# Filling the rotated key columns by a copy at the head of a step, and scaling all 96 key columns on VectorE

## The chip, the cores and the metric

The kernel runs on one core of a Trainium2 chip. Time is the device time of one execution in microseconds (us). Before the change three runs gave 1371.18, 1371.32 and 1372.91 us, a median of 1371.32. Engines are named as in the profile: PE is TensorE's matmul, PEld its weight load, DVE is VectorE, ACT is ScalarE, POOL is GpSimd, and SP is SyncE, which issues the DMAs here.

## The reference

One layer of a mixer: three attention branches and a gate over 2048 tokens of width 1024. The change touches the keys of the latent attention (MLA) alone: 8 heads, each key with 64 columns of its own and 32 rotary columns that all heads share.

```
q  = (rms_norm(cq, q_norm_g) @ w_uq)    # 8 heads x 96
kv = (rms_norm(ckv, kv_norm_g) @ w_ukv) # 8 heads x (64 key + 64 value)
k  = concat([k_nope, k_rope])           # k_rope: 32 columns, one copy for all heads
q, k = rms_norm(q, qn_g), rms_norm(k, kn_g)         # over the 96 columns
q, k = (rope on the last 32 columns of each)
o  = softmax(q k^T / sqrt(96), causal) v
```

The norm divides a whole key by one number, so the rotation of the 32 shared columns can be done once, ahead of the division. What is left for each head and token is to multiply 96 columns by the inverse root: 64 columns that the head owns, and 32 that are the same for all heads up to this factor.

## The kernel before, in words

The work is cut into blocks of 512 tokens (four tiles of 128) and into steps. A step is one block for one group of heads: first the memory branch (m), then the differential branch (d), then the latent branch (a). The sixteen latent steps are named a00 to a33: the first digit is the group of two heads, the second the block of queries.

`prep_a` prepares such a step. Four tiles of matmuls (L838, L842) make q, k and v in PSUM; ACT brings q and the 64 key columns to SBUF (L844, L845), ACT and DVE bring v there. ACT squares, DVE sums the squares (L854, L857) and multiplies the 64 key columns by a gain (L858). POOL then rotates 32 columns of q in place (`rope_in_place`, L354 to L358), adds the sum of squares of the rotary part (L862), adds epsilon (L97) and raises to the power -0.5 (L101); the result is `r_a`, the inverse roots of q and k. POOL also makes the tables for the rotation of the following step (L332 to L335, tile `rt_a`).

With `r_a` the keys are scaled in two pieces: POOL multiplies the shared rotated columns `krot` by the root and writes columns 64 to 95 of the tile `kn_a` (L867), DVE multiplies columns 0 to 63 in place (L871). DVE scales q too (L873). ACT then rounds k and q to f16 (L878, L885), DVE takes the remainder (L879, L886), and SP sends both through a transposing DMA to `kT_a` and `qB_a`, head by head. PE needs these for a first pass that estimates the row maxima (`est_block`, L398) and then for the scores (L917 to L919), whose exponentials ACT makes (L506) and whose low halves DVE makes (L507).

The tiles `kn_a` and `sqq_a` (squares, and space for the rotation) share two buffers, tag `t4`.

Every generator yields costs, and a planner at the end of the function picks the piece that is due next. That sets priorities; a scheduler then decides the order on each engine. Each engine takes its instructions in that order, so one that waits holds up all behind it. Fill work (gates, the output projection of the finished branches, L958 to L961) is spread between the steps in the same manner.

Of the kernel before, what the change touches and what calls it, by code (L numbers as in the profile page):

```python
# [16 lines left out]
ALU = mybir.AluOpType  # L17
# [15 lines left out]
def _bc(ap, axis, n):  # L33
    ap = ap.unsqueeze(axis)
    shape = list(ap.shape)
    shape[axis] = n
    return ap.broadcast_to(shape)
# [3 lines left out]
def hybrid_block(ctx: ExitStack, tc: tile.TileContext, x, mem, positions, norm_g, w_in, mla_q_norm_g,  # L41
# [3 lines left out]
    V, A, G, T, SP = nc.vector, nc.scalar, nc.gpsimd, nc.tensor, nc.sync  # L45
# [15 lines left out]
    def bigt(shape, name):  # L61
        return big.tile(shape, F16, tag="big", name=name)
# [28 lines left out]
    def rstd_of(ss, shape, name, tag="rstd", eps=EPS):  # L91
        r = sm.tile([P, 32 if tag == "rstd" else 8], F32, tag=tag, name=name)
        n = int(np.prod(shape))
        rv = r[:, 0:n]
        if len(shape) == 2:
            rv = rv.rearrange("p (a b) -> p a b", b=shape[1])
        G.tensor_scalar(rv, ss, eps, None, ALU.add)  # L97
        m = mhalf
        if len(shape) == 2:
            m = m.unsqueeze(2)  # L100
        G.tensor_tensor(rv, rv, m.broadcast_to([P] + list(shape)), ALU.pow)  # L101
        return rv
# [96 lines left out]
    def new_qkv(name):  # L199
        return wk.tile([P, 4, 256], F32, tag="qkv", name=name, bufs=2)  # L200

    def tmp4(name):
        return wk.tile([P, 1024], F32, tag="t4", name=name, bufs=2)
# [122 lines left out]
    def rope_tabs(b, g, name):  # L326

        tb = wk.tile([P, 2, 4, 32], F32, tag="rtab", name=f"rt_{name}", bufs=1)
        c = cos_t[:, 4 * b:4 * b + 4, :]
        s = sin_t[:, 4 * b:4 * b + 4, :]  # L330
        g1, g2 = _bc(g[:, 0:16], 1, 4), _bc(g[:, 16:32], 1, 4)
        G.tensor_tensor(tb[:, 0, :, 0:16], c, g1, ALU.mult)  # L332
        G.tensor_tensor(tb[:, 0, :, 16:32], c, g2, ALU.mult)
        G.tensor_tensor(tb[:, 1, :, 0:16], s, g2, ALU.mult)
        G.tensor_tensor(tb[:, 1, :, 16:32], s, g1, ALU.mult)  # L335
        return tb
# [12 lines left out]
    def rope_in_place(q, tb, nh, eng, tmp):  # L349

        tmp = tmp.rearrange("p (t h d) -> p t h d", t=4, d=32)
        C = _bc(tb[:, 0], 2, nh)
        Sn = _bc(tb[:, 1], 2, nh)
        eng.tensor_tensor(tmp[..., 0:16], q[..., 16:32], Sn[..., 0:16], ALU.mult)  # L354
        eng.tensor_tensor(tmp[..., 16:32], q[..., 0:16], Sn[..., 16:32], ALU.mult)
        eng.tensor_tensor(q, q, C, ALU.mult)
        eng.tensor_tensor(q[..., 0:16], q[..., 0:16], tmp[..., 0:16], ALU.subtract)
        eng.tensor_tensor(q[..., 16:32], q[..., 16:32], tmp[..., 16:32], ALU.add)  # L358
# [8 lines left out]
    def put_v(vt, ps):  # L367

        A.activation(vt[:, :, 0:64], ps, AF.Copy, scale=1.0 / WS)
        V.scalar_tensor_tensor(vt[:, :, 65:129], ps, 1.0 / WS, vt[:, :, 0:64], ALU.mult, ALU.subtract)  # L370
# [339 lines left out]
    krot, ss_kr = [], []  # L710
# [108 lines left out]
    def new_v(b, nm):  # L819
        if b in AB:  # L820
            return bigt([P, 4, 2, 130], f"V_{nm}")
        return kvp.tile([P, 4, 2, 130], F16, tag="V", name=f"V_{nm}", bufs=5)

    def prep_a(st):
        g, b, nm = st.g, st.b, st.name
        tb = rope_tabs(b, g_q[:, 64:96], nm)
        q = new_qkv(f"qkv_{nm}")[:, :, 0:192].rearrange("p t (h d) -> p t h d", d=96)
        knt = tmp4(f"kn_{nm}")
        kn = knt[:, 0:768].rearrange("p (t h d) -> p t h d", t=4, d=96)
        vt = new_v(b, nm)  # L830
        G.memset(vt[:, :, :, 64:65], WS)
        for t in range(4):
            ps = ps_p.tile([P, 512], F32, tag="pp", name="pp")
            q0, k0 = 192 * g, 256 * g
            first = True
            for c in range(2):
                for hx, hw in ((0, 0), (0, 1), (1, 0)):
                    T.matmul(ps[:, 0:192], lhsT=lat_q[b][:, t, hx, c, :], rhs=wuq[c][:, hw, q0:q0 + 192], start=first,  # L838
                             stop=False, skip_group_check=True)
                    first = False  # L840
            for i, (hx, hw) in enumerate(((0, 0), (0, 1), (1, 0))):
                T.matmul(ps[:, 192:448], lhsT=lat_kv[b // 2][:, b % 2, t, hx, :], rhs=wukv[0][:, hw, k0:k0 + 256],  # L842
                         start=False, stop=(i == 2), skip_group_check=True)
            A.activation(q[:, t], ps[:, 0:192].rearrange("p (h d) -> p h d", d=96), AF.Copy, scale=1.0 / WS)  # L844
            A.activation(kn[:, t, :, 0:64], ps[:, 192:320].rearrange("p (h d) -> p h d", d=64), AF.Copy, scale=1.0 / WS)  # L845
            put_v(vt[:, t], ps[:, 320:448].rearrange("p (h d) -> p h d", d=64))
            yield 1.6
        sqt = tmp4(f"sqq_{nm}")
        sq = sqt[:, 0:768].rearrange("p (t h d) -> p t h d", t=4, d=96)
        ss = sm.tile([P, 2, 8], F32, tag="ssa", name=f"ss_{nm}")  # L850
        for i, m in enumerate((sqt, knt)):
            sk = m[:, 768:1024].rearrange("p (t h d) -> p t h d", t=2, d=64)
            A.activation(sk, kn[:, 2 * i:2 * i + 2, :, 0:64], AF.Square, scale=1.0 / math.sqrt(96))
            V.reduce_sum(ss[:, 1, 4 * i:4 * i + 4], sk.rearrange("p t h d -> p (t h) d"), axis=AX.X)  # L854
        A.activation(sq, q, AF.Square, scale=1.0 / math.sqrt(96))
        yield 1.0
        V.reduce_sum(ss[:, 0, :], sq.rearrange("p t h d -> p (t h) d"), axis=AX.X)  # L857
        V.tensor_tensor(kn[..., 0:64], kn[..., 0:64], _bc(_bc(g_n, 1, 2), 1, 4), ALU.mult)  # L858
        yield 1.0
        rope_in_place(q[..., 64:96], tb, 2, G, sqt[:, 768:1024])  # L860
        s4 = ss[:, 1, :].rearrange("p (t h) -> p t h", h=2)
        G.tensor_tensor(s4, s4, _bc(ss_kr[b], 2, 2), ALU.add)  # L862
        r = rstd_of(ss.rearrange("p a b -> p (a b)"), [16], f"r_{nm}")
        rq = r[:, 0:8].rearrange("p (t h) -> p t h", h=2)
        rk = r[:, 8:16].rearrange("p (t h) -> p t h", h=2)
        yield 1.0
        G.tensor_tensor(kn[..., 64:96], _bc(krot[b], 2, 2), _bc(rk, 3, 32), ALU.mult)  # L867
        yield 1.0
        yield 1.0
        yield 1.0  # L870
        V.tensor_tensor(kn[..., 0:64], kn[..., 0:64], _bc(rk, 3, 64), ALU.mult)  # L871
        yield 1.0
        V.tensor_tensor(q, q, _bc(rq, 3, 96), ALU.mult)  # L873
        kT = bigt([P, 2, 4, 2, P], f"kT_{nm}") if b in AB else kvp.tile([P, 2, 4, 2, P], F16, tag="kT", name=f"kT_{nm}")
        st.qs, st.qB = [], []
        for h in range(2):
            ks = stack([P, 4, 2, P], f"ks{h}_{nm}")
            A.activation(ks[:, :, 0, 0:96], kn[:, :, h], AF.Copy)  # L878
            lo = V.tensor_tensor(ks[:, :, 1, 0:96], kn[:, :, h], ks[:, :, 0, 0:96], ALU.subtract)  # L879
            with tc.issue_after(lo.ins):  # L880
                V.memset(ks[:, :, :, 96:128], MS)
            SP.dma_start_transpose(kT[:, h].rearrange("p t l k -> p (t l) k"), ks.rearrange("p t l d -> p (t l d)"))
            yield 1.0
            qs = stack([P, 2, 4, P], f"qs{h}_{nm}")
            A.activation(qs[:, 0, :, 0:96], q[:, :, h], AF.Copy)  # L885
            lo = V.tensor_tensor(qs[:, 1, :, 0:96], q[:, :, h], qs[:, 0, :, 0:96], ALU.subtract)  # L886
            with tc.issue_after(lo.ins):
                V.memset(qs[:, :, :, 96:128], 0.0)
            st.qs.append(qs)
            st.qB.append(new_qb([P, 2, 4, P], f"qB{h}_{nm}"))  # L890
            SP.dma_start_transpose(st.qB[h].rearrange("p l t k -> p (l t) k"), qs.rearrange("p l t d -> p (l t d)"))
            yield 1.0
        st.kTs = st.prev.kTs + [kT] if b else [kT]
        st.Vs = st.prev.Vs + [vt] if b else [vt]
        yield 1.0
        yield 1.0
        for h in range(2):
            yield from est_block(st, h, 1, lambda m: st.qs[h][:, 0, :, 96], lambda m, t: st.qB[h][0:96, 0, t, :],
                                 lambda m, c, n: st.kTs[c][0:96, h, 0:n, 0, :])
            SP.dma_start_transpose(st.qB[h][:, 0], st.qs[h][:, 0].rearrange("p t d -> p (t d)"))  # L900
            ready.add((nm, h))
            yield 1.0
# [361 lines left out]
```

## Time and profile before

| what | value |
|---|---|
| median of three runs | 1371.32 us |
| time of the profiled execution | 1372.15 us |
| its span, first to last instruction | 1370.3 us |
| PE busy | 1293.0 us, 94% |
| DVE busy | 1123.1 us, 82% |
| ACT busy | 903.9 us, 66% |
| POOL busy | 333.9 us, 24% |
| mean granted clock of TensorE | 0.989 |

The profiled execution lies 0.83 us above the median, and 1.85 us of it lie outside the span. A busy share is a mean over stages: the latent steps with their preparation lie between about 640 and 1220 us, and the tail after that has no POOL work at all.

### The profile page before, as it was taken

How to read it: one execution, taken by the hardware profiler on the slowest of the kernel's cores; microseconds unless marked ns; L12 is line 12 of the kernel's file. 1: busy time of each engine (PE TensorE's matmuls, PEld its weight loads, DVE VectorE, ACT ScalarE, POOL GpSimd, SP SyncE). 2: the span in 40 equal slices, each digit the busy share in tenths (PEclk: the TensorE clock that was granted, in tenths of full speed). 3: DMA queues.
4: the chain of work that ended last, by engine and by line, in shares of the span. 5: the costliest groups of instructions: out<-in, count | busy, mean ns of one | idle time of the engine just before them, and what ended most of it. 6: DMA issues, size and time to landing. Idle time of an engine off the chain costs nothing.

```text
span 1370.3 us, 35041 instructions
## 1 busy us (share of the span) xinstructions
PE 1293.0 (94%) x13616; PEld 829.5 (61%) x13616; DVE 1123.1 (82%) x2713; ACT 903.9 (66%) x2163; POOL 333.9 (24%) x477
## 2 busy tenths in 40 slices
PE   5988999999999999999998999999999998999998
PEld 2434556667667767667775656666655665655554
DVE  4657888879889867889899889999998998886745
ACT  6656544677878646786896667677766877665521
POOL 2322232403042133113202143223243323200000
PEclk9999999999999999999999999999999999999999
DMA  7998844223113322447446166347525643275452
GB/s 231 199 208 184 184 111 101 59 60 88 41 25 71 79 34 60 78 110 193 124 98 144 40 167 150 84 107 167 109 71 118 145 99 55 40 155 158 141 184 70
DMA packets 294262, 155.52 MB, mean 113 GB/s; under 512 B 239952, under 2 KB 272848, under 8 KB 294096
## 3 DMA queue, kind: packets, MB, share of 16 engines
q1 hardware_dynamic: 294064, 153.29, 47.7%
q8 instruction: 106, 1.74, 0.5%
q14 instruction: 60, 0.49, 0.1%
q0 software_dynamic: 32, 0.00, 0.0%
HBM read 61.75 MB, written 34.34 MB: 70 GB/s over the span
## 4 chain that ended last, share of the span: by engine, by line
PE 56%; DVE 13%; POOL 9%; ACT 8%; DMA 8%; issue 4%; SPq 1%; ACTq 0%; DVEq 0%; POOLq 0%
PE pp L189 6%; PE pp L187 6%; PE pp L188 6%; PE pe L398 5%; DVE plo L507 4%; PE pv L518 3%; PE pv L516 3%; PE pv L536 3%; PE st L572 3%; PE pp L958 3%; PE pp L959 3%; PE pp L960 3%; PE st L917 3%; PE st L918 2%; PE st L919 2%
## 5 line engine op out<-in xcount | busy, mean ns | idle before, releaser
L506 ACT ACTIVATE p<-st 128x512 f32<-128x512 f32 (+3 forms) x672 | 356.2, 551 | 167.2 <-PE st L919 65.8
L507 DVE TENSOR_TENSOR plo<-p 128x512 f16<-128x512 f32 (+3 forms) x672 | 404.6, 615 | 63.1 <-ACT p L506 59.2
L407 ACT ACTIVATE ec<-pe 128x512 bf16<-128x512 f32 (+3 forms) x384 | 197.2, 536 | 39.2 <-PE pe L400 17.1
L516 PEld LDWEIGHTS <-p 128*128 128x128 bf16 x2304 | 186.0, 99 | 51.5 <-DVE y_a L924 4.7
L518 PEld LDWEIGHTS <-p 128*128 128x128 bf16 x2304 | 173.1, 98 | 39.4 <-issue 4.1
L408 DVE TENSOR_TENSOR er<-er,ec 128x512 bf16<-128x512 bf16 (+3 forms) x384 | 141.5, 378 | 29.9 <-ACT ec L407 15.2
L404 ACT ACTIVATE er<-pe 128x512 bf16<-128x512 f32 x192 | 110.0, 606 | 47.2 <-DVE mx_a L413 18.1
L536 PEld LDWEIGHTS <-plo 128*128 128x128 f16 x2304 | 123.1, 97 | 23.7 <-DVE plo L507 5.8
L917 PE MATMUL st<-qB_a,kT_a 97*128 97x512 f16 (+1 forms) x320 | 112.8, 353 | 13.6 <-ACT p L506 8.7
L516 PE MATMUL pv<-V_d,p 128*128 128x65 f16 x1088 | 116.8, 194 | 3.3 <-DVE y_d L579 2.9
L189 PEld LDWEIGHTS <-ht_x 128*128 128x128 f16 x896 | 87.7, 98 | 52.9 <-ACT ht_x L137 3.9
L188 PEld LDWEIGHTS <-ht_x 128*128 128x128 f16 x896 | 87.8, 98 | 47.8 <-issue 4.0
L518 PE MATMUL pv<-V_d,p 128*128 128x64 f16 x1088 | 116.5, 196 | 0.0
L572 PE MATMUL st<-qB_d,kT_d 97*128 97x512 f16 (+1 forms) x320 | 111.4, 353 | 5.2 <-ACT zc L704 2.1
L187 PEld LDWEIGHTS <-ht_x 128*128 128x128 f16 x896 | 87.7, 98 | 47.1 <-issue 2.8
L516 PE MATMUL pv<-V_a,p 128*128 128x65 f16 x1088 | 112.6, 193 | 2.0 <-DVE y_a L924 1.9
L918 PE MATMUL st<-qB_a,kT_a 96*128 96x512 f16 (+1 forms) x320 | 112.6, 352 | 0.0
L398 PE MATMUL pe<-kT_d,qB_d 96*128 96x512 f16 (+2 forms) x320 | 106.2, 348 | 6.8 <-ACT ec L407 3.6
L518 PE MATMUL pv<-V_a,p 128*128 128x64 f16 x1088 | 112.2, 195 | 0.0
L919 PE MATMUL st<-qB_a,kT_a 96*128 96x512 f16 (+1 forms) x320 | 111.9, 350 | 0.0
L398 PE MATMUL pe<-kT_a,qB_a 96*128 96x512 f16 (+2 forms) x320 | 100.0, 349 | 7.7 <-DMA qB_a<-qs_a 4.6
L189 PE MATMUL pp<-w_d,ht_x 128*128 128x512 f16 x256 | 97.0, 379 | 0.0
(293 smaller groups left out, 3337.7 us busy)
## 6 DMA issues: line engine op xcount, KB each, us to landing
xt_x<-in_x_dram SPq DMA_DIRECT2D x16, 512.0 KB, 4.7
xr<-in_x_dram SPq DMA_DIRECT2D x16, 512.0 KB, 3.6
part<-xr SPq DMA_DIRECT2D x16, 512.0 KB, 2.9
ysc<-yt SPq DMA_DIRECT2D x31, 256.0 KB, 2.3
yl<-ysc SPq DMA_DIRECT2D x15, 512.0 KB, 4.6
zsc<-zc SPq DMA_DIRECT2D x48, 128.0 KB, 2.1
xa<-part SPq DMA_DIRECT2D x12, 512.0 KB, 3.6
out_dram<-xa SPq DMA_DIRECT2D x12, 512.0 KB, 2.9
```

Of the source, the lines that this page charges most:

```text
L187: T.matmul(ps[:, :n], lhsT=ht[:, 0, k], rhs=wt[:, 0, :n], start=(k == 0), stop=False)
L188: T.matmul(ps[:, :n], lhsT=ht[:, 0, k], rhs=wt[:, 1, :n], start=False, stop=False)
L189: T.matmul(ps[:, :n], lhsT=ht[:, 1, k], rhs=wt[:, 0, :n], start=False, stop=(k == NK - 1))
L398: T.matmul(ps[:, 0:n], lhsT=lhs(m, t), rhs=rhs(m, c, n // P), start=True, stop=c < b)
L407: A.activation(ec[:, 0:n], ps[:, 0:n], AF.Copy)
L506: A.activation(p32[:, :n], ps[:, :n], AF.Exp, scale=self.scale)
L507: V.tensor_tensor(plo[:, :n], p32[:, :n], phi[:, :n], ALU.subtract)
L516: T.matmul(pvv[:, t, 0:65], lhsT=phi[:, c], rhs=vt[:, 0:65], start=(j == 0 and t == 0), stop=False, skip_group_check=True)
L518: T.matmul(pvv[:, t, 0:64], lhsT=phi[:, c], rhs=vt[:, 65:129], start=False, stop=False, skip_group_check=True)
L536: last["pv"] = T.matmul(pvv[:, t, 0:65], lhsT=plo[:, c], rhs=vt[:, 0:65], start=False, stop=(j == self.njt - 1), skip_group_check=True)
L572: T.matmul(ps[:, :n], lhsT=st.kTs[j // 4][0:97, h, j % 4, m % 2, :], rhs=st.qB[h][0:97, t0:4, m % 2, :], start=True, stop=not diag)
L917: T.matmul(ps[:, :n], lhsT=kt[0:97, h, j % 4, 0, :], rhs=q[0:97, 0, t0:4, :], start=True, stop=False)
```

## The change

POOL no longer multiplies. At the head of a step, behind the memset of the column of ones of v, it copies the 32 rotated columns into columns 64 to 95 of `kn_a` for both heads of the group. Once the roots are there, DVE multiplies all 96 columns in one instruction.

```
         vt = new_v(b, nm)
         G.memset(vt[:, :, :, 64:65], WS)
+        G.tensor_copy(kn[..., 64:96], _bc(krot[b], 2, 2))
         for t in range(4):
...
         yield 1.0
-        G.tensor_tensor(kn[..., 64:96], _bc(krot[b], 2, 2), _bc(rk, 3, 32), ALU.mult)
-        yield 1.0
-        yield 1.0
-        yield 1.0
-        V.tensor_tensor(kn[..., 0:64], kn[..., 0:64], _bc(rk, 3, 64), ALU.mult)
+        yield 1.0
+        yield 1.0
+        yield 1.0
+        V.tensor_tensor(kn, kn, _bc(rk, 3, 96), ALU.mult)
```

The copy is L832 of the changed kernel. Lines from 833 to 866 of the changed kernel are those of before plus one (L862 is L863 there), and from L871 on the numbers are the same again.

The first place is POOL in step a02, from the end of the rotation of q to the roots. `kn_a03` is the key tile of the next step, `rt_a03` its rotation tables, `V_a` tiles of later values. Before:

```order
L358 TENSOR_TENSOR qkv_a02_13501<-qkv_a02_13501,sqq_a02_13667 128x4x2x16
L332 TENSOR_TENSOR rt_a03_14184<-cos_t_113,g_q_119 128x4x16
L333 TENSOR_TENSOR rt_a03_14184<-cos_t_113,g_q_119 128x4x16
L334 TENSOR_TENSOR rt_a03_14184<-sin_t_114,g_q_119 128x4x16
L335 TENSOR_TENSOR rt_a03_14184<-sin_t_114,g_q_119 128x4x16
L862 TENSOR_TENSOR ss_a02_13668<-ss_a02_13668,sskr2_7324 128x8
L831 MEMSET V_a12_16203 128x8
L97 TENSOR_SCALAR r_a02_13735<-ss_a02_13668 128x16
L101 TENSOR_TENSOR r_a02_13735<-r_a02_13735,mhalf_97 128x16
L831 MEMSET V_a20_17646 128x8
L867 TENSOR_TENSOR kn_a02_13502<-krot2_7357,r_a02_13735 128x8x32
```

The same stretch of POOL in the changed kernel:

```order
L358 TENSOR_TENSOR qkv_a02_13501<-qkv_a02_13501,sqq_a02_13668 128x4x2x16
L332 TENSOR_TENSOR rt_a03_14184<-cos_t_113,g_q_119 128x4x16
L333 TENSOR_TENSOR rt_a03_14184<-cos_t_113,g_q_119 128x4x16
L334 TENSOR_TENSOR rt_a03_14184<-sin_t_114,g_q_119 128x4x16
L335 TENSOR_TENSOR rt_a03_14184<-sin_t_114,g_q_119 128x4x16
L863 TENSOR_TENSOR ss_a02_13669<-ss_a02_13669,sskr2_7324 128x8
L832 COPY kn_a03_14190<-krot3_7698 128x8x32
L97 TENSOR_SCALAR r_a02_13736<-ss_a02_13669 128x16
L831 MEMSET V_a12_16203 128x8
L101 TENSOR_TENSOR r_a02_13736<-r_a02_13736,mhalf_97 128x16
L831 MEMSET V_a20_17646 128x8
```

The multiplication behind the roots is gone, and the copy for step a03 stands ahead of the roots of step a02. It stands so (the copy for the next step ahead of L101 of this one) in eleven of the sixteen steps: a00 to a21, and a32. In a22, a23, a30, a31 and a33 no copy stands in that stretch.

The second place is DVE around the scaling in the same step; `plo` are low halves of exponentials, `xr` rows of the output projection, `rl` and `y_d` belong to the end of a differential step. Before:

```order
L507 TENSOR_TENSOR plo_13705<-p32_13704 128x512
L526 RECIPROCAL rl_13752<-pv_13099 128x4
L871 TENSOR_TENSOR kn_a02_13502<-kn_a02_13502,r_a02_13735 128x8x64
L873 TENSOR_TENSOR qkv_a02_13501<-qkv_a02_13501,r_a02_13735 128x4x192
L507 TENSOR_TENSOR plo_13744<-p32_13743 128x384
L581 TENSOR_SCALAR rl_13752<-rl_13752,neglam_132 128x4
L879 TENSOR_TENSOR ks0_a02_13805<-kn_a02_13502,ks0_a02_13805 128x4x96
```

DVE in the changed kernel:

```order
L507 TENSOR_TENSOR plo_13679<-p32_13678 128x128
L961 SCALAR_TENSOR_TENSOR xr3_13693<-pp_13770,xr3_13693 128x512
L871 TENSOR_TENSOR kn_a02_13502<-kn_a02_13502,r_a02_13736 128x768
L873 TENSOR_TENSOR qkv_a02_13501<-qkv_a02_13501,r_a02_13736 128x4x192
L507 TENSOR_TENSOR plo_13706<-p32_13705 128x512
L526 RECIPROCAL rl_13753<-pv_13100 128x4
L879 TENSOR_TENSOR ks0_a02_13805<-kn_a02_13502,ks0_a02_13805 128x4x96
```

L871 is one instruction over 768 elements instead of 512, and the low half and the reciprocal that stood ahead of it now stand behind L873. Small moves of this kind run through the order of PE, ACT and DVE over all latent steps, and the fill work moves with them.

## Rows read from the trace of the kernel before

**Rows 1.** The page, busy time by engine (us, share of the span, instructions).

```profile
PE 1293.0 (94%) x13616; PEld 829.5 (61%) x13616; DVE 1123.1 (82%) x2713; ACT 903.9 (66%) x2163; POOL 333.9 (24%) x477
```

**Rows 2.** Windows: stretch, length, busy (instructions) by engine, granted clock, DMA share, GB/s.

```profile
core 0: us, PE busy (x) PEld busy (x) DVE busy (x) ACT busy (x) POOL busy (x), PEclk, DMA share, GB/s
640.00:1220.00 580.00, 546.14 (x6394) 364.58 (x6393) 524.51 (x1291) 425.09 (x1040) 162.59 (x223) 0.98 0.48 111
1220.00:1370.00 150.00, 144.64 (x1270) 78.29 (x1266) 89.64 (x183) 54.52 (x107) 0.00 (x0) 1.00 0.47 143
745.00:775.00 30.00, 24.91 (x384) 17.68 (x382) 26.36 (x72) 23.73 (x58) 0.13 (x1) 0.89 0.27 47
1035.00:1050.00 15.00, 12.46 (x106) 6.83 (x105) 11.17 (x27) 6.59 (x17) 6.84 (x10) 0.77 0.66 94
```

**Rows 3.** Waits of PE, 640 to 1370 us: total us, times, longest us.

```profile
PE st L917 <- ACT p L506: 8.7, 13, 2.5
PE pe L398 <- DMA qB_a<-qs_a: 4.6, 3, 2.0
PE st L917 <- DMA qB_a<-qs_a: 4.3, 4, 1.5
```

**Rows 4.** Chain that ended last, 786 to 800 us (step a02): start us, us, what.

```profile
787.09 2.94 POOL r_a L101
790.04 0.02 issue
790.06 0.04 DVE kn_a L871
...
790.67 1.22 DVE qkv_a L873
...
795.84 3.50 DMA qB_a<-qs_a
...
799.39 0.66 PE pe L398 x3
```

**Rows 5.** Timeline of POOL, 783.5 to 791.5 us: start us, us, instruction [idle].

```profile
784.18 0.91 POOL L358 TENSOR_TENSOR qkv_a<-qkv_a,sqq_a 128x128 f32<-128x128 f32 x1
...
786.40 0.19 POOL L862 TENSOR_TENSOR ss_a<-ss_a,sskr 128x8 f32<-128x8 f32 x1
...
786.75 0.26 POOL L97 TENSOR_SCALAR r_a<-ss_a 128x16 f32<-128x16 f32 x1
787.09 2.94 POOL L101 TENSOR_TENSOR r_a<-r_a,mhalf 128x16 f32<-128x16 f32 x1
...
790.11 1.12 POOL L867 TENSOR_TENSOR kn_a<-krot,r_a 128x256 f32<-128x256 f32 x1
```

**Rows 6.** Timeline of DVE in the same step.

```profile
790.06 0.69 DVE L871 TENSOR_TENSOR kn_a<-kn_a,r_a 128x512 f32<-128x512 f32 x1 [0.39 <-POOL r_a L101]
790.67 1.37 DVE L873 TENSOR_TENSOR qkv_a<-qkv_a,r_a 128x768 f32<-128x768 f32 x1
```

**Rows 7.** Timeline of DVE in step a23, with POOL idle.

```profile
1054.50 0.95 DVE L873 TENSOR_TENSOR qkv_a<-qkv_a,r_a 128x768 f32<-128x768 f32 x1
```

**Rows 8.** Lines: group, count, busy us, mean ns, idle before and its releaser.

```profile
L873 DVE TENSOR_TENSOR qkv_a<-qkv_a,r_a 128x768 f32<-128x768 f32 x16 | 19.2, 1201 | 0.0
...
L867 POOL TENSOR_TENSOR kn_a<-krot,r_a 128x256 f32<-128x256 f32 x16 | 17.5, 1096 | 0.9
...
L871 DVE TENSOR_TENSOR kn_a<-kn_a,r_a 128x512 f32<-128x512 f32 x16 | 11.7, 730 | 7.1 <-POOL r_a L101 7.0
...
L462 POOL MEMSET s_d<- 128x256 f16 x32 | 9.5, 310 | 60.9 <-DVE zc L705 16.1 <-DMA qB_m<-qa_m 16.0 <-issue 10.6
```

**Rows 9.** Source L867: shortest, median and longest of its instructions, in ns.

```profile
L867 POOL TENSOR_TENSOR kn_a<-krot,r_a x16: 728/1122/1328, 682.0 to 1183.9; 128x256 f32<-128x256 f32 x16
```

**Rows 10.** Source L332, the first of the table products: shortest, median, longest, ns.

```profile
L332 POOL TENSOR_TENSOR rt_a<-cos_t,g_q x16: 318/700/777, 628.3 to 1138.2; 128x64 f32<-128x64 f32 x16
```

**Rows 11.** Waits of ACT, 640 to 1370 us: total us, times, longest us.

```profile
ACT ks_a L878 <- POOL kn_a L867: 13.2, 10, 3.0
```

## The prediction

> **What bounds the kernel now.** I read the busy times first: PE is busy for 1293.0 of 1370.3 us, DVE for 1123.1, POOL for 333.9 [rows 1]. So time is lost where PE waits or where its clock is low, and the question is whether the edited chain does either. The windows come second [rows 2]. From 640 to 1220 us, where all sixteen latent steps are prepared, PE is busy for 546.1 of 580 us and DVE for 524.5; in the tail POOL does nothing, so the edit can't act there except by what it leaves behind. [...] At full speed the windows would have taken 30 x 0.11 = 3.3 us and 15 x 0.23 = 3.5 us less.
>
> Third, the waits of PE [rows 3]: 4.6 us in three waits of the estimate (L398) for the transposed queries, 4.3 us in four waits of the scores for the same DMA, and 8.7 us in thirteen waits for exponentials, the longest 2.5 us. These 17.6 us are all that a shorter or longer preparation can act on directly. The chain of waits shows one such place whole, step a02 [rows 4]: roots on POOL, L871 and L873 on DVE, then ACT and DVE work, the DMA of `qB_a` and the estimate on PE at 799.39. There, what comes before L101 counts in full. The timeline of POOL [rows 5] shows that POOL works without a pause from the rotation (L358) to the roots: what is put in between makes the roots late by its own length.
>
> **What the change removes.** L867 ran right behind the roots, beside L871 and L873. The timelines show that this cost DVE time: L871 takes 0.69 us, POOL's L867 starts 0.05 us after it and takes 1.12 us, and L873, which starts while L867 runs, takes 1.37 us [rows 5, 6]; with POOL idle the same L873 takes 0.95 us [rows 7]. Alone L867 takes 0.73 us, its median is 1.12 [rows 9]. So the first to start goes at its own pace and the other waits for it. [...]
>
> The sum on DVE: L873 has a mean of 1.201 us over sixteen [rows 8], so the collisions cost it 16 x (1.201 - 0.945) = 4.1 us, which go. L871 grows from 512 to 768 elements. That is the shape of L873, so 0.945 us instead of a mean of 0.730 [rows 7, 8]: 16 x 0.215 = 3.4 us, which come. DVE gains 0.7 us, which is nothing among 1123.
>
> On the path behind the roots, in a02: before, keys were ready when L867 ended, 791.23, that is 1.17 us after L871 started, and queries when L873 ended, 1.98 us after it. Afterwards keys need 0.95 us and queries 0.95 + 0.95 - 0.08 (the overlap of the two rows) = 1.82 us. So both come 0.2 us sooner after the roots.
>
> **What the change adds.** A copy of 128x256 per step. It is not shown in this trace. It must take at least as long as a memset of as many elements, which reads nothing, 0.31 us [rows 8], and at most as long as L867, which reads twice, 0.73 us alone and 1.12 us in its median with DVE beside it [rows 9]. I take the middle of the two undisturbed values, 0.52, and add something for collisions: of the small table products that stand in the same stretch of POOL the shortest takes 0.32 and the median 0.70 us [rows 10]; half of this difference gives 0.7 us in all. [...]
>
> The place decides more than the length. The buffers make it: the next step's `kn_a` takes the buffer in which q was just rotated, so its copy can't start before L358 of this step. In the new order of POOL it therefore stands, in eleven of sixteen steps, between the tables and L101, ahead of the roots of the step before. Queued behind it are L97 and L101, and for them wait L871 on DVE (7.0 us of waiting already [rows 8]) and all that stands behind L871. So in eleven steps keys and queries come 0.7 - 0.2 = 0.5 us later than before; in the other five 0.2 us sooner. The bounds per step are 0.31 - 0.2 = +0.1 and 1.12 - 0.2 = +0.9 us.
>
> What of it reaches the end? If all of it did: 11 x 0.5 - 5 x 0.2 = +4.5 us. If PE always had other work: nothing. PE waited for the transposed queries before an estimate three times [rows 3], and I count those three: +1.5 us, with bounds of 3 x 0.1 = +0.3 and 11 x 0.9 - 1.0 = +8.9 us. In the other steps the cover is fill work of the output projection and the preceding scores on PE; where that cover is used up the step counts too. The ACT wait for L867, 13.2 us in ten waits [rows 11], isn't a gain of its own: it now ends with L871, by the same roots, and is in the sum by the 0.2 us.
>
> Against the profiled execution, 1372.15 us, this is 1373.6; that execution lies 0.83 us above the median of the three runs, and a median goes into the forecast: 1371.32 + 1.5 = 1372.8 us.
>
> **Rivals.** First, faster. The key side no longer needs POOL, the collision at L873 is gone, and ACT, whose exponentials stand behind L878, is held up less. For a gain beyond the 0.2 us per step one of the low-clock places must go: at 1035 to 1050 us PE waits up to 2.5 us for exponentials and 3.5 us are lost to the clock [rows 2, 3]. Step a22 is prepared there, one of the five with no copy ahead of its roots. Price: 1371.3 - 2.5 - 3.5 = 1365.3 us, or with 0.5 to 1.5 us of late roots elsewhere about 1366.5. For it: the windows show the spot; against it: 0.2 us is small against 2.5, so only the moved order could do it.
>
> Second, slower. Late roots add a long PE wait and a low-clock stretch. Its place is a02: PE waits at the end of the chain in rows 4, and the wait grows by the copy. From the point where a wait is followed by a low clock, as beside 752 us (PE waits 2.0 us [rows 3], clock 0.89 [rows 2]), it costs 3.3 to 3.5 us more. Time: 1372.8 + 3.4, and one more step on the path with 0.5 to 1 us, about 1377. For it: eleven delayed steps and DVE, which stands in order behind the roots, at 90% in this stage; against it: only three of sixteen estimates waited at all.
>
> Third, nothing: the copy is short, both 0.2 us savings meet it, and PE covers the rest: 1371.3 us. It shares its outcome with my forecast.
>
> The order of the fill work moves on PE, DVE and ACT over all steps. That is not a term that I can sum; it acts by waits and low-clock spots of the size above, in either direction, and is why the range is wider than the sum.
>
> **How the numbers follow.** A change is told from none at about 0.2%, 2.7 us: faster is below 1368.6, slower above 1374.1. My forecast together with the third rival gets 0.38 (within 0.2%). Slower, by late roots or by order, gets 0.34. Faster gets 0.28. The likeliest case's own range is 1370 to 1375. The range 1367.0 to 1379.0 reaches to 1366.5 of the first rival almost and past 1377 of the second, and takes in most of the +0.3 to +8.9 us of the sum; about 0.1 is left out on each side.
>
> **What would show it.** Right: L873 at 0.95 us in every step; L871 at about 0.95; the copy at 0.5 to 0.9 us between the tables and L97; ACT's L878 released by L871 on DVE; DVE's wait at L871 for the roots up from 7.0 us to 10 or more; the PE wait for `qB_a` longer by about 0.5 us at a02. Wrong: a copy of 1.1 us or more, or L871 slowed beyond 1 us by another POOL read, would mean a collision that I priced too low; DVE waits at L871 no longer than before would mean that the order made room for the copy, and the first or third rival holds. If the count of low-clock stretches between 640 and 1220 us changes, the size comes from order and not from the terms above.

## The result, and the profile after

The changed kernel takes 1386.66 us in the median of four runs (1383.81 to 1388.34), the kernel before 1372.12 us beside it: a ratio of 1.0097 with an interval of [1.0068, 1.0126]. It is slower, by about 14 us, and outside the range of the forecast. The profiled execution took 1386.20 us with a span of 1384.5, so it stands for the median.

Busy times hardly move. The page of the changed kernel, answering to [rows 1]:

```profile
PE 1298.9 (94%) x13616; PEld 832.6 (60%) x13616; DVE 1121.5 (81%) x2713; ACT 903.2 (65%) x2163; POOL 325.7 (24%) x477
```

DVE has 1.6 us less to do, POOL 8.2 us less, and PE 5.9 us more of busy time for the same matmuls, at a mean granted clock of 0.984 (0.989 before). The windows of the changed kernel, with the columns of [rows 2]:

```profile
640.00:1220.00 580.00, 539.25 (x6265) 360.50 (x6262) 510.85 (x1261) 412.71 (x1017) 157.41 (x222) 0.97 0.47 108
1220.00:1370.00 150.00, 148.34 (x1394) 82.87 (x1391) 95.11 (x207) 67.30 (x133) 0.00 (x0) 1.00 0.47 140
745.00:775.00 30.00, 24.72 (x374) 17.27 (x371) 26.46 (x71) 23.54 (x57) 0.00 (x0) 0.89 0.31 50
1035.00:1050.00 15.00, 15.00 (x177) 9.65 (x175) 14.96 (x36) 10.16 (x24) 6.84 (x10) 1.00 0.64 130
1100.00:1200.00 100.00, 89.08 (x1021) 56.55 (x1021) 85.34 (x216) 70.58 (x164) 26.23 (x34) 0.91 0.36 72
```

In the latent stage, 640 to 1220 us, PE does 6.9 us less in the same 580 us than before, DVE 13.7 us less, and the clock is 0.97 for 0.98. Of the two spots that the forecast had marked, 745 to 775 us is as before (a granted clock of 0.89). In 1035 to 1050 us PE now runs without a pause at a clock of 1.00 (0.77 before), but the kernel is some 9 us late by then (counted in matmuls), and a spot like it comes later: from 1055 to 1075 us the clock is 0.83 (1.00 before). In the 100 us from 1100 it is 0.91, so 9 us of full-speed work are lost in that stretch alone; before it was 0.97 there, 3 us.

Waits of PE in the changed kernel, 640 to 1370 us, as in [rows 3]:

```profile
PE st L917 <- ACT p L506: 11.3, 13, 2.4
PE pe L398 <- ACT ec L407: 7.2, 12, 1.3
PE st L917 <- DMA qB_a<-qs_a: 6.5, 4, 2.4
PE pe L398 <- DMA qB_a<-qs_a: 3.7, 3, 2.5
```

The estimate's wait for the transposed queries, on which the forecast rested, went from 4.6 to 3.7 us. At a02, where the forecast had looked for 0.5 us more, it fell from 1.29 to 0.55 us (PE's timeline, before and after):

```profile
799.39 0.66 PE L398 MATMUL pe<-kT_a,qB_a 96*128 96x512 f16 x3 [1.29 <-DMA qB_a<-qs_a]
```

```profile
804.28 0.66 PE L398 MATMUL pe<-kT_a,qB_a 96*128 96x512 f16 x3 [0.55 <-DMA qB_a<-qs_a]
```

The waits for exponentials (8.7 to 11.3), of the scores for queries (4.3 to 6.5) and of the estimate for its own copies on ACT (1.3 us in four before, now 7.2 in twelve) grew.

What the edit does to its own instructions came out close to what was worked out. Its three lines as groups (as in [rows 8]), and the copy's shortest, median and longest in ns (as in [rows 9]):

```profile
L871 DVE TENSOR_TENSOR kn_a<-kn_a,r_a 128x768 f32<-128x768 f32 x16 | 15.8, 985 | 14.9 <-POOL r_a L101 14.9
L873 DVE TENSOR_TENSOR qkv_a<-qkv_a,r_a 128x768 f32<-128x768 f32 x16 | 15.7, 981 | 0.0
...
L832 POOL COPY kn_a<-krot 128x256 f32<-128x256 f32 x16 | 10.9, 683 | 0.0
```

```profile
L832 POOL COPY kn_a<-krot x16: 388/540/1159, 634.8 to 1155.0; 128x256 f32<-128x256 f32 x16
```

L873 fell from 1.201 to 0.981 us, L871 grew to 0.985, the copy's median is 0.54 us, its mean 0.68. The wait of DVE for the roots doubled, from 7.0 to 14.9 us. POOL in step a02, answering to [rows 5]:

```profile
788.29 0.90 POOL L358 TENSOR_TENSOR qkv_a<-qkv_a,sqq_a 128x128 f32<-128x128 f32 x1
...
790.73 0.40 POOL L832 COPY kn_a<-krot 128x256 f32<-128x256 f32 x1
791.21 0.32 POOL L97 TENSOR_SCALAR r_a<-ss_a 128x16 f32<-128x16 f32 x1
...
791.65 2.93 POOL L101 TENSOR_TENSOR r_a<-r_a,mhalf 128x16 f32<-128x16 f32 x1
```

The copy stands between the rotation (L358) and the roots (L101), as the order had it. And ACT's L878 now waits for L871, about as long as it waited for L867 [rows 11]:

```profile
ACT ks_a L878 <- DVE kn_a L871: 12.3, 10, 3.3
```

So the edited instructions did what was expected, and the sum was still wrong. Two explanations were tested: "late roots" (the copies make the roots late, and the end sees it) and "order" (the edit makes the scheduler put other work in another place, and that costs).

### The profile page after: what moved, and what is told of

The parts are those of the page before. It is cut to its first block, busy times and chain, and to the rows that moved or that the text cites. A ratio compares the mean times of both kernels' runs of the same rounds, so it can differ in the third digit from the quotient of the medians.

```text
span 1384.5 us, 35034 instructions
## 1 busy us (share of the span) xinstructions
PE 1298.9 (94%) x13616; PEld 832.6 (60%) x13616; DVE 1121.5 (81%) x2713; ACT 903.2 (65%) x2163; POOL 325.7 (24%) x477
## 4 chain that ended last, share of the span: by engine, by line
PE 52%; DVE 14%; DMA 10%; POOL 9%; ACT 8%; issue 5%; SPq 1%; ACTq 0%; DVEq 0%; POOLq 0%
PE pp L187 6%; PE pp L189 6%; PE pp L188 6%; PE pe L398 5%; DVE plo L507 4%; PE pv L518 3%; PE pv L516 3%; PE pv L536 3%; PE st L572 3%; PE pp L958 3%; PE pp L960 3%; PE pp L959 3%; DMA qB_a<-qs_a 2%; PE st L917 2%; PE st L918 2%
## 5 line engine op out<-in xcount | busy, mean ns | idle before, releaser
L507 DVE TENSOR_TENSOR plo<-p 128x512 f16<-128x512 f32 (+3 forms) x672 | 405.4, 616 | 69.3 <-ACT p L506 65.3
L917 PE MATMUL st<-qB_a,kT_a 97*128 97x512 f16 (+1 forms) x320 | 114.6, 358 | 18.0 <-ACT p L506 11.3
L398 PE MATMUL pe<-kT_a,qB_a 96*128 96x512 f16 (+2 forms) x320 | 103.2, 355 | 11.2 <-ACT ec L407 6.7
```

Source lines behind the costliest of these rows:

```text
L398: T.matmul(ps[:, 0:n], lhsT=lhs(m, t), rhs=rhs(m, c, n // P), start=True, stop=c < b)
L507: V.tensor_tensor(plo[:, :n], p32[:, :n], phi[:, :n], ALU.subtract)
L917: T.matmul(ps[:, :n], lhsT=kt[0:97, h, j % 4, 0, :], rhs=q[0:97, 0, t0:4, :], start=True, stop=False)
```

## The experiments

Each ratio below is against the kernel before, run beside it on the same chip (medians 1372.4 to 1373.3 us).

**Four kernels in whatever order the scheduler gave them.** The first doubles the copy, so that roots are still later:

```diff
         G.tensor_copy(kn[..., 64:96], _bc(krot[b], 2, 2))
+        G.tensor_copy(kn[..., 64:96], _bc(krot[b], 2, 2))
```

> The changed kernel with the copy issued twice, so that POOL spends about another 0.54 us ahead of the roots in the same eleven steps. By chance the scheduler then leaves the other engines almost in the order of before: a matmul of PE stands 5 places from its place before on average, against 20 in the changed kernel. Theory late roots (the 14 us of the change come from the roots that the copy delays): the delay per step rises from about 0.5 to 1.0 us, so the loss grows too, 1395 to 1405 us. Theory order (the 14 us come from the order that the scheduler chose for PE, DVE and ACT when the copy made its plan late): with the order of before the loss nearly goes, 1372 to 1378 us, in spite of the longer delay.

It took 1369.75 us, 0.9982 [0.9969, 0.9996]. With two copies ahead of the roots the loss is gone.

The second puts a memset in the place of the copy (it leaves out the rotated part of the keys):

```diff
-        G.tensor_copy(kn[..., 64:96], _bc(krot[b], 2, 2))
+        G.memset(kn[..., 64:96], 0.5)
```

> The changed kernel with a memset of the same 128x256 elements in the place of the copy; it leaves out the rotated part of the keys, and stands at the same places on POOL as the copy. The order of the other engines stays near that of before (4.5 places for a matmul of PE). Theory late roots: the memset takes 0.31 instead of 0.54 us, so a bit over half of the loss stays, 1377 to 1382 us. Theory order: 1371 to 1374 us.

1372.15 us, 1.0000 [0.9981, 1.0018].

The third ties the copy behind the roots of the step before:

```diff
-        G.tensor_copy(kn[..., 64:96], _bc(krot[b], 2, 2))
+        if roots:
+            with tc.issue_after(roots[-1].ins):
+                G.tensor_copy(kn[..., 64:96], _bc(krot[b], 2, 2))
+        else:
+            G.tensor_copy(kn[..., 64:96], _bc(krot[b], 2, 2))
...
+        roots.append(last_root[-1])
```

Here `last_root` collects the instructions of L101; the lines that fill it are left out.

> The changed kernel with the copy for a step held on POOL behind the roots of the step before, with all else of the change kept (96 columns on VectorE). The order of the other engines is near that of before (6 places for a matmul of PE). Roots come as early as before, keys and queries 0.2 us sooner. Theory late roots: 1369 to 1372 us, the loss is gone because the copy is out of the way. Theory order: 1369 to 1374 us as well, so this run tests whether either is enough, and whether there is a gain to be had; if 96 columns on VectorE were the cause, it would stay near 1386 us.

1378.88 us, 1.0047 [1.0031, 1.0063], though no copy stands ahead of its step's roots here.

The fourth has no edit and makes the roots late by a memset:

```diff
+        G.memset(sqt[:, 0:512], 1.0)
         r = rstd_of(ss.rearrange("p a b -> p (a b)"), [16], f"r_{nm}")
```

> The kernel before, with a memset of 128x512 f32 elements (about 0.53 us, from the 0.31 us of 256) on POOL ahead of the roots of every latent step, into a tile that is no longer read. Nothing else of the change is in it; the order of the other engines stays near that of before (5 places for a matmul of PE). Theory late roots: sixteen steps later by 0.5 us, 1380 to 1390 us. Theory order: 1372 to 1376 us.

1381.18 us, 1.0071 [1.0053, 1.0090]. Taken together the four make no line: two copies gain, none ahead of the roots loses. DVE's waits for the roots (7.0 us before, 14.9 in the changed kernel) are 6.5, 10.6, 17.9 and 11.3 us in the four: with the copy behind the roots they are the longest of all. This doesn't rule out late roots. In each kernel the order of 13616 matmuls and some 5000 other instructions had moved as well, so none of the four has one change in it.

**The same work in a fixed order.** From here the order was taken out of the comparison: in each kernel the instructions of PE, DVE, ACT and SP are tied, one behind the other, in the order that another kernel has; GpSimd, where the edit is, stays free. (The kernel before was not run tied to its own order; a tied kernel at 1.0001 below shows that the ties themselves cost nothing that can be measured.) The traces of the tied kernels show the order given, instruction by instruction, on PE, DVE and ACT. The edit to each file is this, with a table of places behind it:

```diff
-    out_tail()
+    out_tail(); pin(tc)
...
+        for a, b in zip(ins, ins[1:]):
+            tc.add_manual_dep(b, a.name, mybir.DependencyInfo(mybir.DependencyClass.NoSync,
+                                                              mybir.DependencyReason.DATA), reason="order")
```

> The changed kernel, with the order of PE, DVE, ACT and SP tied to the order of the kernel before by issue-order edges; GpSimd's own order is left free, and the copy stands ahead of the roots of the step before in 12 steps (11 in the changed kernel). Theory order (the loss is in the new order of the fill work and scores, not in the edit): 1370 to 1376 us, as the kernel before in this job. Theory late roots (the copy makes roots late, and that is what the end sees): 1383 to 1389 us, as the changed kernel, since every copy and all 96 columns on DVE are still there.

The edit in the order of before: 1377.0 us, 1.0039 [1.0020, 1.0057]. Neither theory had it: about 40% of the loss is the edit's own.

> The kernel before, none of the edit in it, with PE, DVE, ACT and SP tied to the order that the changed kernel has. Theory order: 1382 to 1390 us, a loss of 10 us or more without the edit. Theory late roots: 1370 to 1376 us, since no copy stands on GpSimd. A value midway, 1376 to 1382, would mean that order and edit each carry a part.

No edit, the order of the changed kernel: 1382.24 us, 1.0071 [1.0052, 1.0090]. The larger part is the order's alone. The two parts make 1.10% together, the changed kernel had 0.97 [0.68, 1.26].

**The edit's own part is late roots.** Two kernels test it, one without the edit and with late roots (the memset above with 768 columns), one with the edit and without late roots (the copy tied behind the roots as above), both in the order of before.

> The kernel before, with a memset of 768 columns (an estimate of 0.9 us from 0.31 us for 256) on GpSimd ahead of the roots in each of the 16 latent steps, and all of PE, DVE, ACT and SP tied to the order of the kernel before: the price of late roots alone in one fixed order. Theory order: late roots are covered in most steps; three steps count, 3 x 0.9 = 2.7 us, 1373 to 1378 us. Theory late roots: most steps count, 16 x 0.9 = 14 us, 1383 to 1389 us.

> The edit in the order of the kernel before (on PE, DVE, ACT and SP), with the copy tied behind the roots of the step before, so that it makes no roots late; the copy itself and the 96 columns on DVE are still there. Theory late roots (in a fixed order every us that DVE waits longer for the roots reaches the end; the edit in this order lost 4.7 us with 6.0 us more of such waits): the wait of DVE for the roots falls from 13.0 back to about 7 us, and the time to 1370 to 1374 us. Theory width (the 96 columns and the copy's collisions cost the 4.7 us): 1375 to 1379 us.

The first took 1382.74 us, 1.0078 [1.0059, 1.0097]; the second 1373.73 us, 1.0001 [0.9988, 1.0015]. The wait of DVE for the roots in 640 to 1370 us (total, times, longest), first in the kernel before, then in the edit in the order of before, then with the copy behind the roots, then with the memset (lines move: L871 is L879 and L872 in the last two):

```profile
DVE kn_a L871 <- POOL r_a L101: 7.0, 11, 1.2
```

```profile
DVE kn_a L871 <- POOL r_a L101: 13.0, 13, 1.8
```

```profile
DVE kn_a L879 <- POOL r_a L103: 6.4, 9, 1.1
```

```profile
DVE kn_a L872 <- POOL r_a L101: 16.3, 14, 2.5
```

Set against the times, 6.0 us more of this wait went with 0.39% (5.3 us), 0.6 us less with nothing, 9.3 us more with 0.78% (10.7 us). So in this order the loss is about as long as the added wait. The clean pair is the edit with the copy ahead of the roots and behind them, since nothing differs but the place of the copy (all other instructions stand in the same order in both traces, on GpSimd too): 0.39% against 0.01%. The 96 columns and the copy itself cost nothing that can be measured (at most 0.15% by the interval). The memset takes 0.73 us, and 16 of them are 11.7 us, nearly all of which was lost:

```profile
L863 POOL MEMSET sqq_a<- x16: 728/732/737, 677.5 to 1193.6; 128x768 f32 x16
```

But it isn't a clean witness of late roots alone: it writes a buffer of the tag `t4`, and ACT's copies of the next keys (L845) waited for it twice, 4.5 us in all.

The wait doesn't show on PE as a wait for keys or queries. With the memset PE's waits (as in [rows 3]; the line numbers are one higher) are:

```profile
PE st L918 <- ACT p L506: 15.7, 14, 3.3
PE st L918 <- DMA qB_a<-qs_a: 4.2, 4, 1.6
```

Queries are waited for as before (4.3), exponentials 15.7 us for 8.7. The way there is seen on ACT: L878, which rounds the keys, waits for them, and the exponentials of the step in hand stand behind it in the same queue. In the clean pair, first the edit with the copy ahead of the roots, then behind them (L886 is L878 there, L925 is L917):

```profile
ACT ks_a L878 <- DVE kn_a L871: 20.4, 13, 3.4
PE st L917 <- ACT p L506: 11.2, 14, 2.5
```

```profile
ACT ks_a L886 <- DVE kn_a L879: 15.1, 13, 3.0
PE st L925 <- ACT p L508: 6.6, 10, 2.5
```

ACT's wait for the keys is 5.3 us shorter with the copy behind the roots, PE's for exponentials 4.6 us, and the kernel 0.38%. What is late is the step in hand, not the one that is prepared. Behind L871 on DVE the differences (L507) of the step in hand stand too; how much comes by that way was not measured.

The other direction, with a product in the place of the power, so that the roots come sooner:

```diff
-        r = rstd_of(ss.rearrange("p a b -> p (a b)"), [16], f"r_{nm}")
+        r = rstd_of(ss.rearrange("p a b -> p (a b)"), [16], f"r_{nm}", eps=4e-3, add=ALU.mult, op=ALU.mult)
```

(`rstd_of` takes its two operations as parameters for this; those lines are left out.)

> The kernel before in its own order, with a product in place of the power in the roots of the latent steps (leaves out the inverse root there), an estimate of 0.3 us in place of 2.93 us: roots some 2.6 us sooner in 16 steps. Theory late roots: the 7.0 us that DVE waits for the roots go, and as with late roots each us reaches the end: 1364 to 1368 us. If only lateness beyond that of the kernel before costs: 1370 to 1374 us.

> The same fast roots (the inverse root left out), without the edit, in the order of the changed kernel. If the order costs its 9.9 us by making the roots wait (DVE waits for them 11.7 us there, 7.0 in the order of before): most of the loss goes, 1366 to 1371 us, within 3 us of the fast roots in the order of before. If it costs by other waits (DVE for ACT's halves of the keys at L879, 10.7 against 3.0 us): 1372 to 1378 us, 7 to 10 us above the fast roots in the order of before.

In the order of before: 1361.23 us, 0.9927 [0.9901, 0.9953], about 10 us below before, where 7.0 us of waits were there to take (the expectation had 1364 to 1368 us, and the 3 us beyond the wait are not explained); in the order of the changed kernel: 1373.56 us, 0.9998 [0.9980, 1.0015]. The roots took 0.22 us for 2.93:

```profile
L101 POOL TENSOR_TENSOR r_a<-r_a,mhalf x16: 209/218/660, 678.2 to 1173.6; 128x16 f32<-128x16 f32 x16
```

The distance between the two orders stays (0.71%, as with slow roots). So the order does not act through the roots, though DVE waits longer for them in it: the first of the two readings failed, and the second (1372 to 1378 us, by other waits) holds.

**Where the order costs.** The waits of PE and DVE in the kernel without the edit in the changed kernel's order:

```profile
PE st L917 <- ACT p L506: 8.4, 10, 2.4
PE pe L398 <- ACT ec L407: 8.2, 12, 2.0
PE st L917 <- DMA qB_a<-qs_a: 6.5, 4, 2.4
PE pe L398 <- DMA qB_a<-qs_a: 3.9, 3, 2.5
```

```profile
DVE kn_a L871 <- POOL r_a L101: 11.7, 12, 1.9
DVE ks_a L879 <- ACT ks_a L878: 10.7, 8, 2.9
```

They are close to those of the changed kernel, but for 3 us less each of waits for exponentials and for the roots: 8.2 us of the estimate's waits for its copies (1.3 before), 6.5 us of the scores' for queries, 10.7 us of DVE for ACT's halves of the keys (2.8 before). To find the place, the changed kernel's order was used up to a given matmul and the order of before behind it, still without the edit:

> The kernel before, without the edit, in the order of the changed kernel up to its 7770th matmul (about 800 us, step a03) and in the order of before behind it. The whole of that order cost 9.9 us. If the loss is spread over the stage: about 4 us, 1374 to 1379 us (the lag at 800 us was 4.7 us in the kernel that has this order throughout). If it is one place late in the stage (1060 to 1160 us, with its waits of the estimate for its copies): 1370 to 1374 us. If the early part alone makes it: 1380 to 1385 us.

> The kernel before, without the edit, in the order of the changed kernel up to its 9300th matmul (about 940 us) and in the order of before behind it. Up to 800 us that order cost nothing (0.9991), the whole of it 9.9 us. If the loss lies between 800 and 940 us: 1380 to 1384 us. If it is spread over what follows 800 us: 1374 to 1378 us. If it lies behind 940 us: 1369 to 1374 us.

> The same with the order of the changed kernel up to its 10838th matmul (about 1090 us). If the loss lies in the last steps, behind 1085 us (the waits of the estimate for its copies and the short low-clock stretches there): 1369 to 1374 us. If it is spread over what follows 800 us: 1377 to 1381 us. If it lies ahead of 1085 us: 1380 to 1384 us.

They took 1371.2 us, 0.9991 [0.9975, 1.0008]; 1376.87 us, 1.0041 [1.0021, 1.0061]; and 1375.27 us, 1.0012 [0.9995, 1.0030]. With the last steps alone in the old order, all but 0.12% of the 0.71% is gone. That doesn't put the loss behind 1085 us, and the parts don't simply add. The starts of single matmuls in the traces (one execution each; with the same order up to the 9300th matmul, three of them differ by up to 4.7 us there) show where it arises. The 10838th starts at 1085.2 us in the kernel before, at 1092.7 in the changed kernel's order without the edit and at 1095.7 in the changed kernel: 7.5 of 12.0 us and 10.5 of 14.4 us are lost by then. In the second of the three kernels the loss comes behind the change of order: its 9300th matmul starts 2.0 us late, its 9800th 6.9, so its 0.41% says little of the order ahead of 940 us. The other halves:

> The kernel before, without the edit, in its own order up to its 10838th matmul (1085 us) and in the order of the changed kernel behind it: the other half of before_in_edit_order_to_1085 (1.0012). If the last steps make the loss by their order alone: 0.5 to 0.7% above before, 1379 to 1383 us, with more PE waits for the copies of the estimate (L398) and short low-clock stretches at 1130 to 1230 us. If they cost only behind the other order's first part: 1370 to 1376 us.

> The changed kernel in its own order up to the 10838th matmul and in the order of before behind it, the copies where they are. If late roots (4.7 us in the order of before) and the order of the last steps (about 8 us) add up, the second part goes: 1376 to 1381 us, 0.3 to 0.6% above before. If the loss behind 1085 us comes from the lateness that the copies have made by then, it stays: 1383 to 1389 us.

The first, 1383.9 us, 1.0079 [1.0053, 1.0106], agrees but is no clean witness: where the two orders meet PE waits once for 4.4 us and once for 2.1 us in the estimate, which the changed kernel doesn't do there (PE in that kernel, 1080 to 1260 us):

```profile
PE pe L398 <- ACT er L404: 4.5, 2, 4.4
...
PE pe L398 <- ACT ec L407: 3.3, 4, 2.1
```

The second has no such wait: the changed kernel, copies and late roots in it, with only the steps behind 1085 us in the old order, took 1377.1 us, 1.0034 [1.0018, 1.0050]. That is close to the 0.39% of late roots in the order of before, though the changed kernel's order up to 1085 us is in it too. Its 10838th matmul is 10.5 us late, as in the changed kernel; from there the old order takes back 5.5 us, and the new one adds 3.9. What went with the last steps' order is seen in their windows, first the changed kernel, then the one with the old order there:

```profile
1085.00:1250.00 165.00, 149.24 (x1749) 95.37 (x1746) 140.26 (x360) 117.53 (x269) 27.36 (x35) 0.95 0.41 86
```

```profile
1085.00:1250.00 165.00, 151.70 (x1843) 97.40 (x1840) 146.48 (x373) 119.36 (x273) 29.20 (x35) 1.00 0.46 99
1100.00:1200.00 100.00, 91.63 (x1148) 59.16 (x1147) 94.65 (x234) 77.47 (x179) 29.20 (x35) 1.00 0.36 75
```

At a clock of 0.95 the first loses 165 x 0.05 = 8 us of full-speed work to the low clock; the second loses none. The kernel before loses 3 us, and that it doesn't in the second is part of what the old order takes back:

```profile
1085.00:1250.00 165.00, 151.66 (x1758) 94.36 (x1757) 142.48 (x361) 114.62 (x258) 30.17 (x36) 0.98 0.50 104
```

PE's waits in the same 165 us, changed kernel first:

```profile
PE st L917 <- DMA qB_a<-qs_a: 6.5, 4, 2.4
PE st L917 <- ACT p L506: 4.5, 3, 2.4
PE pe L398 <- ACT ec L407: 1.9, 5, 0.6
```

```profile
PE st L917 <- DMA qB_a<-qs_a: 3.9, 4, 1.2
...
PE st L917 <- ACT p L506: 1.7, 2, 1.3
...
PE pe L398 <- ACT ec L407: 0.5, 2, 0.3
```

The longest of these waits fell from 2.4 to 1.3 us. On ACT, which makes exponentials and halves of keys in one queue, L878 waits 7.0 us for transfers to free the halves' buffer in the new order, 2.8 in the old:

```profile
ACT ks_a L878 <- DMA qB_a<-qs_a: 7.0, 4, 2.9
```

```profile
ACT ks_a L878 <- DMA qB_a<-qs_a: 2.8, 3, 1.7
```

In the new order ACT has the first two of the four tiles of the next step's projection (L845, L846, L369) five exponentials earlier than in the old one (around 1105 us), and these exponentials of the step in hand stand behind them. That this one displacement makes the waits was not tried by itself.

**A version below both.** The order that came with two copies was tried with the single copy, without the edit, and with the copy behind the roots:

> The changed kernel (one copy), tied on PE, DVE, ACT and SP to the order that the kernel with two copies had (1369.75 us, 0.9982 of the kernel before). Theory order: it follows that order, 1366 to 1373 us, the lower end if one copy less helps. Theory late roots: 1383 to 1389 us, as the changed kernel.

> The kernel before, without the edit, in the order (PE, DVE, ACT, SP) of the kernel with two copies, in which the edit reached 1367.3 us. Theory order (this order is better by itself): 1363 to 1369 us, by 3 to 5 us below the edit's, as in the order of before. Theory edit (in an order that suits it the edit gains): 1371 to 1375 us, as the kernel before in its own order.

> The edit in the order of the kernel with two copies, with the copy tied behind the roots of the step before. Theory late roots: in that order the waits of DVE for the roots are 4.4 us, so there is little to take away: 1364 to 1368 us. Theory width: no change, 1366 to 1369 us. If it is slower than 1369 us, a copy that comes later delays something that neither theory has.

1367.26 us, 0.9957 [0.9942, 0.9972]; 1367.8 us, 0.9952 [0.9935, 0.9969]; 1367.76 us, 0.9958 [0.9942, 0.9974]. All three beat both kernels, and equally: the gain is the order's, the edit brings nothing. The 3 to 5 us that the edit was expected to cost here are not seen. In this order DVE waits little for the roots, without the edit and with it:

```profile
DVE kn_a L871 <- POOL r_a L101: 1.8, 3, 0.9
```

```profile
DVE kn_a L871 <- POOL r_a L101: 4.4, 7, 1.3
```

So 2.6 us more of this wait cost nothing that can be measured here: what a late root costs depends on the order too. The gain lies ahead of 1085 us: the 10838th matmul starts at 1080.2, 1077.2 and 1078.8 us in the three (1085.2 before). In 1085 to 1250 us their clock is 0.95 or 0.96, as low as the changed kernel's, so a low clock in that stretch alone doesn't make a kernel slow. Without the edit:

```profile
1085.00:1250.00 165.00, 152.69 (x1727) 93.81 (x1724) 139.09 (x347) 113.61 (x253) 28.31 (x36) 0.95 0.45 102
```

## Why the prediction was wrong

Its prices were right. L871 and L873 are at 0.985 and 0.981 us where it had 0.945, the copy is at 0.54 us in its median and 0.68 in its mean where it had 0.52 clear and 0.7 with collisions, the copy stands in 11 steps ahead of the roots, L878 is released by L871, and DVE waits for the roots 14.9 us, as "10 or more" would have it.

The first step that failed is "I count those three: +1.5 us". It took from all that stands behind L871 on DVE only the estimate's waits for queries. In a fixed order the edit cost 5.3 us (0.39%), about the sum that the prediction gives for "If all of it did", +4.5 us, and dismisses; the copy tied behind the roots takes it all away. Its own words "all that stands behind L871" were the right list. DVE is 90% busy in this stage [rows 2], and in the traces of the tied kernels its instructions stand in the order given; it sat idle at L871 for 13.0 us with the edit (7.0 before), and everything behind L871 waited with it. ACT's wait for the keys at L878, which the prediction set aside as "in the sum by the 0.2 us", went from 14.6 us (13.2 for L867, 1.4 for L871) to 20.4 in the fixed order, and exponentials stand behind it. The cover that it named, fill work on PE, covered late queries (4.6 to 5.0 us and 4.3 to 4.3 us of waits in the fixed order) but not late exponentials (8.7 to 11.2).

The second, larger failure is the order of the fill work, "not a term that I can sum", for which it allowed a few us in either direction. Alone it cost 0.71%, 9.9 us between the medians. No price from the trace of before gives this, but the runs give the width: one work in three orders made 0.9952, 1 and 1.0071. A range of 6 us on either side was too narrow for a change that moves the order. Its last test, on the low clock between 640 and 1220 us, pointed at this part: the clock is 0.98 before and with the edit in the old order, 0.97 in the changed kernel and in its order without the edit. It did not separate the two causes, since about 40% of the loss came from late roots.

Of the rivals, the slower one (1377 us by late roots and a low-clock stretch) had the late roots right. That late roots alone made 1377.0 us too is luck: 3.4 us of its sum were a low-clock stretch, and the clock of 640 to 1220 us stayed at 0.98 with the edit in the old order. Its place was wrong: at a02 PE's wait for queries fell in the changed kernel (1.29 to 0.55 us), and the clock is 1.00 there before and after (785 to 806 and 790 to 811 us).

What stays open: which displacements make the new order's loss, of which 7.5 us in one execution arose ahead of 1085 us, and why the old order behind 1085 us takes part of the lateness back.

## What to carry to other kernels

When a scheduler sets the order, a small edit is two changes, the work and the order; fix the order (each engine's instructions tied to the old sequence) before reading anything from a variant. Order alone made 0.5% less and 0.7% more in this kernel. When a wait is added on an engine that is 90% busy and takes its instructions in a given order, count it in full, for all that is queued behind it, until the trace shows slack there (here 6.0 us more of it went with 5.3 us); slack of the one result that the edit concerns is not enough. (In the order that came with two copies 2.6 us more of it cost nothing.) An order found by accident can be kept: here it was worth 0.4 to 0.5%.

## What the runs showed of the hardware

A copy of 128x256 f32 on GpSimd took 0.39 us at its shortest, 0.54 in its median and 1.16 at its longest (L832 in the changed kernel).

Some instructions of GpSimd and DVE took longer side by side. In the kernel before, L873 took 1.37 us in the nine steps in which it started while L867 ran, 1.07 in the two in which it started ahead of L867 (a table product, L335, still ran beside it there), and 0.94 to 0.95 in the other five; L867 took 1.33 us in those two steps, against 0.73 at its shortest. In the changed kernel L873 is at 0.95 us in its median. The copy takes stretching instead: four of the sixteen (1010 to 1109 us) stand behind the roots, beside L873, and take 1.12 us each, against 0.39 at the shortest; L873 takes 1.07 us there. A copy beside L961 took 0.39 us (at 982.86 us), so not every pair does this, and why some do was not measured.

In the kernel before, the granted clock was 0.50 from 1040 to 1046 us and 1.00 from 1047 to 1050, which makes most of the 0.77 of the window from 1035 to 1050 us.

The power on 128x16 took 2.93 us in its median (L101 in the kernel before), a product of the same shape 0.22 us (with the fast roots, in the order of before).
